# The opening of a transformer layer on TensorE: matmuls in the order the program is written, against an order chosen by a scheduler

## The chip, the cores and the metric

The kernel runs on one core of a Trainium2 chip. The core has a matrix engine (TensorE, PE in the profile), a vector engine (DVE), a scalar engine (ACT), GpSimd (POOL) and SyncE (SP), which here only issues DMA transfers. Each engine works off its own list of instructions in order and waits on semaphores for the others. The metric is the device time of one execution in microseconds. Three runs of the kernel before took 2039.68, 2039.70 and 2042.13 us, median 2039.7 us.

## The reference

One layer of a hybrid model over 256 latent tokens `x` and 256 context tokens `ctx`, model width 2048, everything in fp32. Cut to what bears on this case:

```
mod_x = split(silu(c)     @ w_mod + b_mod, 6)      # shift, scale, gate, ... for x
mod_c = split(silu(c_ctx) @ w_mod + b_mod, 6)      # the same for ctx
modulate(x, g, shift, scale) = rms_norm(x, g) * (1 + scale) + shift
h   = modulate(x,   g_mix, mod_x[0], mod_x[1])
hc  = modulate(ctx, g_mix, mod_c[0], mod_c[1])
qa, ka, va, qb, kb, vb, rb, lrf, lrb, gate_a, gate_b = split(h  @ w_in, ...)
...                                             split(hc @ w_in, ...)
o_attn = windowed attention(qa, ka, va, context keys and values)
o_gla  = chunked bidirectional gated linear attention(qb, kb, vb, gates; starts from context end states)
x = x + mod_x[2] * (sigmoid(gate_a) * (o_attn @ w_attn_o) + sigmoid(gate_b) * (o_gla' @ w_gla_o)) @ w_out
x = x + mod_x[5] * conv_ffn(modulate(x, g_ffn, mod_x[3], mod_x[4]))
```

The modulation of each token by shift and scale needs the matrix product `silu(c) @ w_mod` first, and it needs the whole row of a token for the rms. So the first projection of `h` waits for both.

## The kernel before

**Numbers.** An fp32 operand is split into a high part and the rest (`hi` by ACT, `lo` by DVE), and each product is three matmuls: hi by hi, lo by hi, hi by lo. A weight tile of two k-tiles (256 rows by 512 columns, 512 KB) comes by a load into a `raw` buffer; `wsplit` (L156) makes `whi` (ACT) and `wlo` (DVE, 128x1024) from it.

**The opening**, about 213 us, runs from the start to the first gated-linear-attention (GLA) work. First `c` and `c_ctx` (`crow`) go through SiLU and a transpose (`pc`, L97). `load_tokens` (L356) loads the two 128-token tiles of a stream, sums squares (ACT L368 for the first tile, DVE L366 for the second, both into `junk`) and transposes them on TensorE (`ptx`, L373) into `xr`; the copies out of PSUM alternate between ACT (L378) and DVE (L376). `rms_scale` and `token_rows` turn the sums into a factor per token (DVE L330 to L344 with `dg` last, TensorE `pr` L345, ACT `rrow` L347). `mod_both` (L229) makes shift and scale for some k-tiles of both streams: 1 MB tiles of `w_mod` (`mraw`), matmuls `pm` (L245), a DVE transpose `mtr` (L248), a small matmul `pcol` (L250), four copies (L253), the bias (L256). `affine_group` (L398) makes `h` for some k-tiles: scale (L400), then for each k-tile DVE `xr` (L394), ACT hi (L395), DVE lo (L396). In names such as `h10lo` the first digit is the stream (0 is x, 1 is ctx).

The projections are made in groups of k-tiles, (first k-tile, count): (0,2), (2,2), (4,4), (8,4), (12,4). In each group the program writes: affine of x; the GLA queries of x in two blocks of 512 columns (QB, by `proj_T` L186); affine of ctx; the GLA keys of both streams (KB, `proj_T`); the values of both (VB, `proj_nat` L163). The partial sums of the groups are added up in `qb0`, `kb0` and `vb0` by `add_to` (L406): an ACT copy in the first group (L410), a DVE addition (L412) in the later ones. The modulation of the next group is cut into steps, and `tick()` (L133) takes one now and then at the rate `bg_rate`.

**What sets the order.** Loads on SP are chained in the order they are written (L66). On the compute engines a scheduler of the framework orders the instructions by a priority that follows the order of writing, and by what it expects to be ready; the weight splits have a high priority (L158). So the order in which the code is written is not the order on an engine.

**After the opening** come the columns of the convolution weights (L449 to L452), the low-rank gate projection (`plr`), the last block of GLA keys beside the first GLA head, then the heads, attention, the merge and the ConvFFN.

Of the kernel before, what the change touches and what calls it, by code (L numbers as in the profile page):

```python
# [30 lines left out]
def layer_kernel(ctx, tc, A, out):  # L31
# [44 lines left out]


    x00 = M("x00", [P, D])
    nc.sync.dma_start(x00, A["x"][0][0:P, :])
# [22 lines left out]
    def columns(name, parts, eng=G):  # L102
        rows = sm.tile([P, P], F32, name="rows", tag="t128", bufs=2)
        n = 0
        for ap in parts:
            k = ap.shape[0] // P
            eng.dma_start(rows[n:n + k, :], ap.rearrange("(k p) -> k p", p=P))
            n += k
        pt = bank("pt_" + name, (P, P))
        PE.transpose(pt[:, :n], rows[:n, :], ident[:n, :n])  # L110
        t = cst.tile([P, n], F32, name=name)
        V.tensor_copy(t, pt[:, :n])
        return t

    c1 = columns("c1", [A["b_mod"][0], A["g_mix"][0], A["g_ffn"][0]], nc.scalar)
    bmod, gmix, gffn = c1[:, 0:96], c1[:, 96:112], c1[:, 112:128]


    bg_steps = []
# [13 lines left out]
    def tick():  # L133
# [3 lines left out]
        while later and later[0][0] < 0:  # L137
            later.pop(0)[1]()
# [16 lines left out]

    def wsplit(src):  # L156
        raw = wload(src)
# [7 lines left out]
    def proj_nat(w, r0, c0, kts, lhs, evac):  # L165

        banks = [acc.tile([P, 512], F32, name="acc", tag="acc") for _ in lhs]
        for k0 in kts[::2]:
            tick()
            nk = min(2, kts[-1] + 1 - k0)  # L170
            hi, lo = wsplit(w[r0 + k0 * P:r0 + (k0 + nk) * P, c0:c0 + 512])
            for i, l in enumerate(lhs):
                for k in range(nk):
                    kt = k0 + k
                    ahi, alo = l(kt)
                    PE.matmul(banks[i], ahi, hi[:, k, :], start=(kt == kts[0]), stop=False)  # L176
                    PE.matmul(banks[i], alo, hi[:, k, :], start=False, stop=False)  # L177
            for i, l in enumerate(lhs):
                for k in range(nk):
                    kt = k0 + k  # L180
                    PE.matmul(banks[i], l(kt)[0], lo[:, k, :], start=False, stop=(kt == kts[-1]))  # L181
# [3 lines left out]
    def proj_T(w, c0, kts, rhs, evac):  # L185
# [4 lines left out]
        for k0 in kts[::2]:  # L190
            tick()
            nk = min(2, kts[-1] + 1 - k0)
            hi, lo = wsplit(w[k0 * P:(k0 + nk) * P, c0:c0 + 512])
            for part in range(2):
                for f in range(4):
                    for k in range(nk):
                        kt = k0 + k
                        w_ = (lo if part else hi)[:, k, f * P:(f + 1) * P]
                        for i, r in enumerate(rhs):
# [3 lines left out]
                            PE.matmul(o, w_, ahi, start=(kt == kts[0] and b == 0 and part == 0),  # L203
                                      stop=(kt == kts[-1] and part == 1), skip_group_check=True)
                            if part == 0:
                                PE.matmul(o, w_, alo, start=False, stop=False, skip_group_check=True)  # L206
        for i in range(len(banks)):
            evac(i, banks[i])
# [22 lines left out]
    def mod_both(part, t0, n, dst):  # L231
# [5 lines left out]
        def step(k0):  # L237
# [8 lines left out]
            if k0 == KT - nk:  # L246
                tr = W2("fb", "mtr", [P, n, 4, 32])
                V.transpose(tr.rearrange("p a b c -> p (a b c)"), a[0])  # L248
                pc = bank(f"pcol{part}_{t0}", (32, n * 4, 2))
                PE.matmul(pc, sel[:, 0:32], tr.rearrange("p a b c -> p (a b) c")[:, :, 0:2], start=True, stop=True)  # L250
                pv = pc.rearrange("p (a b) c -> p b c a", b=4)
                for b4 in range(4):
                    V.tensor_copy(dst[32 * b4:32 * b4 + 32, :, t0:t0 + n], pv[:, b4, :, :])  # L253
                b0 = part * 16 + t0
                d = dst[:, :, t0:t0 + n]
                V.tensor_tensor(d, d, bmod[:, b0:b0 + n].unsqueeze(1).to_broadcast([P, 2, n]), op=ALU.add)  # L256

        return [lambda k0=k0: step(k0) for k0 in range(0, KT, nk)]
# [92 lines left out]
    groups = [(0, 2), (2, 2), (4, 4), (8, 4), (12, 4)]  # L351
    mods = [mod_both(0, t0, n, shift1) + mod_both(1, t0, n, scale1) for t0, n in groups]
# [4 lines left out]

    def load_tokens(s):
        ss = sm.tile([P, 2], F32, name="ss0", tag="ss0", bufs=2)
        for t in range(2):  # L360
            x_ = x00
            if s or t:
                x_ = M(f"x{s}{t}", [P, D])
                load(x_, A["ctx" if s else "x"][0][t * P:(t + 1) * P, :])
            if t:
                V.scalar_tensor_tensor(junk, x_, 1.0, x_, op0=ALU.mult, op1=ALU.mult, accum_out=ss[:, t:t + 1])  # L366
            else:
                S.activation(junk, x_, AF.Square, accum_out=ss[:, t:t + 1])  # L368
            for g in range(4):
                pt = bank("ptx", (P, 4, P), side=True)  # L370
                for k in range(4):
                    kt = g * 4 + k
                    PE.transpose(pt[:, k, :], x_[:, kt * P:(kt + 1) * P], ident)  # L373
                dst = xr[2 * s + g // 2][:, (g % 2) * 4:(g % 2) * 4 + 4, t * P:(t + 1) * P]
                if g % 2:
                    V.tensor_copy(dst, pt)  # L376
                else:
                    S.activation(dst, pt, AF.Copy)  # L378
        rrow1.append(token_rows("fa", f"rrow{s}", rms_scale(ss, D, [P, 2])))
# [35 lines left out]
    hh, hl = [], []  # L415
    for gi, (t0, n) in enumerate(groups):
        kts = ALL[t0:t0 + n]
        if gi == 0:
            load_tokens(0)
            for f in mods[0]:  # L420
                f()
        while bg_steps:
            bg_steps.pop(0)()
        if gi + 1 < len(groups):
            bg_steps.extend(mods[gi + 1])
# [613 lines left out]
```

## Time and profile before

| | |
|---|---|
| median of three runs | 2039.7 us |
| the profiled execution's own time | 2039.47 us |
| its span in the trace | 2037.7 us |
| TensorE busy | 1979.4 us (97%) |
| DVE busy | 1430.0 us (70%) |
| ACT busy | 960.7 us (47%) |
| granted TensorE clock, mean | 0.991 |
| end of group (0,2) and of the opening in the trace | 62.98 us and 213.08 us |

The profile is of one execution. Times in the trace count from the start of the span, which is 1.8 us shorter than the execution's own time. Matmuls are pipelined, so the durations of single matmuls overlap, and the distance between two starts is what one costs. A granted clock of 1.00 is 2.4 GHz and 0.50 is 1.2 GHz. Where a row says `[3.23 <-DVE dg L344]`, the engine was idle for 3.23 us before it, and that instruction ended the wait.

### The profile page before, as it was taken

How to read it: one execution, taken by the hardware profiler on the slowest of the kernel's cores; microseconds unless marked ns; L12 is line 12 of the kernel's file. 1: busy time of each engine (PE TensorE's matmuls, PEld its weight loads, DVE VectorE, ACT ScalarE, POOL GpSimd, SP SyncE). 2: the span in 40 equal slices, each digit the busy share in tenths (PEclk: the TensorE clock that was granted, in tenths of full speed). 3: DMA queues.
4: the chain of work that ended last, by engine and by line, in shares of the span. 5: the costliest groups of instructions: out<-in, count | busy, mean ns of one | idle time of the engine just before them, and what ended most of it. 6: DMA issues, size and time to landing. Idle time of an engine off the chain costs nothing.

```text
span 2037.7 us, 27395 instructions
## 1 busy us (share of the span) xinstructions
PE 1979.4 (97%) x10384; PEld 1647.3 (81%) x10384; DVE 1430.0 (70%) x2237; ACT 960.7 (47%) x1394; POOL 38.9 (2%) x62
## 2 busy tenths in 40 slices
PE   6999999999999999999999999899999999999998
PEld 4778888888787777787778888788888888888887
DVE  4657577887758888877775455788887555667754
ACT  4323464553345656444334444565555434556532
POOL 0001000001000000000000000000000000000000
PEclk8999999999999999999999999899999999999999
DMA  9977223345544456788886665577776656555563
GB/s 350 364 259 224 91 77 93 93 135 192 172 146 129 124 184 206 263 271 272 273 269 220 237 207 187 193 248 251 261 245 207 212 193 193 188 187 187 193 211 111
DMA packets 214340, 413.54 MB, mean 203 GB/s; under 512 B 12548, under 2 KB 21092, under 8 KB 213184
## 3 DMA queue, kind: packets, MB, share of 16 engines
q1 hardware_dynamic: 212320, 406.89, 60.5%
q0 software_dynamic: 1360, 4.74, 0.8%
q8 instruction: 81, 1.33, 0.3%
q14 instruction: 51, 0.42, 0.1%
q10 hardware_dynamic: 528, 0.17, 0.0%
HBM read 409.63 MB, written 2.11 MB: 202 GB/s over the span
## 4 chain that ended last, share of the span: by engine, by line
PE 78%; DVE 10%; DMA 8%; ACT 2%; issue 2%; DVEq 0%; POOL 0%; ACTq 0%; SPq 0%
PE acc L176 13%; PE acc L177 13%; PE acc L181 13%; PE acc L219 8%; PE accs L219 8%; DMA raw<-in_w_mod 8%; PE acc L223 4%; PE accs L223 4%; PE acc L203 3%; DVE wlo L62 3%; DVE macc L284 3%; PE acc L206 2%; PE pm L245 1%; PE pa L552 1%; ACT whi L61 1%
## 5 line engine op out<-in xcount | busy, mean ns | idle before, releaser
L61 ACT ACTIVATE whi<-raw 128x1024 fp32r<-128x1024 f32 x568 | 600.9, 1059 | 784.7 <-PE acc L177 500.7
L62 DVE TENSOR_TENSOR wlo<-raw,whi 128x1024 fp32r<-128x1024 f32 x568 | 694.1, 1226 | 335.4 <-ACT whi L61 302.6
L284 DVE SCALAR_TENSOR_TENSOR macc<-raw,ccol,macc 128x512 f32<-128x512 f32 x240 | 180.3, 751 | 110.5 <-DMA raw<-in_w_mod 107.0
L219 PE MATMUL acc<-h,whi 128*128 128x512 f32 x704 | 178.6, 396 | 2.2 <-DVE h L396 2.2
L219 PE MATMUL accs<-h,whi 128*128 128x512 f32 x704 | 176.3, 392 | 0.0
L219 PEld LDWEIGHTS acc<-h,whi 128*128 128x128 f32 x704 | 127.8, 191 | 25.6 <-DVE h L396 2.5
L219 PEld LDWEIGHTS accs<-h,whi 128*128 128x128 f32 x704 | 126.6, 189 | 22.6
L176 PE MATMUL acc<-whi,h00hi 128*128 128x512 f32 x352 | 141.2, 401 | 1.5 <-DVE kb L412 0.6
L176 PE MATMUL acc<-whi,h01hi 128*128 128x512 f32 x352 | 139.8, 397 | 0.0
L177 PE MATMUL acc<-whi,h00lo 128*128 128x512 f32 x352 | 139.8, 397 | 0.0
L177 PE MATMUL acc<-whi,h01lo 128*128 128x512 f32 x352 | 137.7, 391 | 0.0
L177 PE MATMUL acc<-whi,al 128*128 128x512 f32 x352 | 137.1, 389 | 0.0
L176 PE MATMUL acc<-whi,ah 128*128 128x512 f32 x352 | 137.0, 389 | 0.0
L223 PEld LDWEIGHTS acc<-h,wlo 128*128 128x128 f32 x704 | 97.0, 192 | 7.1
L223 PEld LDWEIGHTS accs<-h,wlo 128*128 128x128 f32 x704 | 96.0, 190 | 6.9
L223 PE MATMUL acc<-h,wlo 128*128 128x256 f32 x704 | 99.1, 284 | 0.0
L181 PE MATMUL acc<-wlo,h00hi 128*128 128x512 f32 x352 | 98.0, 394 | 0.2 <-DVE wlo L62 0.2
L223 PE MATMUL accs<-h,wlo 128*128 128x256 f32 x704 | 98.2, 282 | 0.0
L181 PE MATMUL acc<-wlo,h01hi 128*128 128x512 f32 x352 | 97.0, 393 | 0.0
L181 PE MATMUL acc<-wlo,ah 128*128 128x512 f32 x352 | 94.4, 389 | 0.0
L176 PEld LDWEIGHTS acc<-whi,h00hi 128*128 128x128 f32 x352 | 66.9, 190 | 15.6 <-ACT kb L410 0.7
L181 PEld LDWEIGHTS acc<-wlo,h00hi 128*128 128x128 f32 x352 | 65.8, 189 | 14.4 <-DVE wlo L62 1.0
(375 smaller groups left out, 3461.5 us busy)
## 6 DMA issues: line engine op xcount, KB each, us to landing
raw<-in_w_in SPq DMA_DIRECT2D x208, 512.0 KB, 4.1
raw<-in_w_up SPq DMA_DIRECT2D x176, 512.0 KB, 3.6
raw<-in_w_mod SPq DMA_DIRECT2D x128, 512.0 KB, 4.0
raw<-in_w_down SPq DMA_DIRECT2D x88, 512.0 KB, 3.7
mraw<-in_w_mod SPq DMA_DIRECT2D x32, 1024.0 KB, 11.9
raw<-in_w_attn_o SPq DMA_DIRECT2D x32, 512.0 KB, 4.5
raw<-in_w_gla_o SPq DMA_DIRECT2D x32, 512.0 KB, 4.7
raw<-in_w_out SPq DMA_DIRECT2D x32, 512.0 KB, 3.6
```

Of the source, the lines that this page charges most:

```text
L61: S.activation(hi, src, AF.Copy)
L62: V.tensor_tensor(lo, src, hi.bitcast(F32), op=ALU.subtract)
L176: PE.matmul(banks[i], ahi, hi[:, k, :], start=(kt == kts[0]), stop=False)
L177: PE.matmul(banks[i], alo, hi[:, k, :], start=False, stop=False)
L181: PE.matmul(banks[i], l(kt)[0], lo[:, k, :], start=False, stop=(kt == kts[-1]))
L203: PE.matmul(o, w_, ahi, start=(kt == kts[0] and b == 0 and part == 0), stop=(kt == kts[-1] and part == 1), skip_group_check=True)
L206: PE.matmul(o, w_, alo, start=False, stop=False, skip_group_check=True)
L219: PE.matmul(banks[f], hi[:, k, f * P:(f + 1) * P], pair(k0 + k), start=(k0 + k == kts[0]), stop=False, skip_group_check=True)
L223: PE.matmul(banks[f][:, 0:T], lo[:, k, f * P:(f + 1) * P], pair(k0 + k)[:, 0, :], start=False, stop=(k0 + k == kts[-1]), skip_group_check= ...
L245: PE.matmul(a[0][q:q + 32, :], cS[:, kt, :], raw[:, k, :], start=(kt < 4), stop=(kt >= 12))
L284: V.scalar_tensor_tensor(a[0], raw[:, k, :], ccol[:, kt:kt + 1], a[0], op0=ALU.mult, op1=ALU.add)
L552: PE.matmul(pa[:, t, :], k2[:, dt, t * P:(t + 1) * P], q2[:, dt, tq * P:(tq + 1) * P], start=(dt == 0), stop=(dt == 1))
```

## The change

The opening's matmuls are put on TensorE in the order in which the code is written (`tc.manual_schedule` for PE alone, closed behind the last group); the other engines are still ordered by the scheduler. The written order is new too:

- the two tiles of x are loaded first and in one chain, and both are transposed before the modulation;
- the end of a modulation (`pcol`, copies, bias) is a step of its own, and 34 transposes of the identity into an otherwise unused PSUM bank (`warm`, `keep_busy`) are written between the steps of the first modulation;
- the weight tiles of the first QB blocks, and of the first VB and KB, are loaded ahead (`early`);
- the context is loaded before the first QB, and transposed behind it;
- VB stands before KB, and KB is last in every group;
- the groups are (0,2), (2,2), (4,2), (6,2), (8,4), (12,4): one more than before;
- `tick()` is called after every 6 or 12 matmuls instead of every weight tile, and `proj_nat` takes the four token tiles in two pairs;
- the first of the four convolution columns (`cw0`) moves ahead of the last group.

```diff
+    order = ExitStack()
+    order.enter_context(tc.manual_schedule(engines={mybir.EngineType.PE}))
...
-        while later and later[0][0] < 0:
-            later.pop(0)[1]()
+        due = [e for e in later if e[0] < 0]
+        later[:] = [e for e in later if e[0] >= 0]
+        for e in due:
+            e[1]()
...
     def wsplit(src):
-        raw = wload(src)
+        raw = early.pop(0) if early else wload(src)
...
+            step = 2 if fine[0] else len(lhs)
+            for i2 in range(0, len(lhs), step):
+                for part in range(2):
+                    for i in range(i2, min(i2 + step, len(lhs))):
...
+                            if fine[0] and mms % 6 == 0 and mms < len(lhs) * nk * 3:
+                                tick()
...
-    groups = [(0, 2), (2, 2), (4, 4), (8, 4), (12, 4)]
-    mods = [mod_both(0, t0, n, shift1) + mod_both(1, t0, n, scale1) for t0, n in groups]
+    groups = [(0, 2), (2, 2), (4, 2), (6, 2), (8, 4), (12, 4)]
+    def both_parts(t0, n):
+        (s0, e0), (s1, e1) = (mod_both(part, t0, n, dst) for part, dst in ((0, shift1), (1, scale1)))
+        if n == 4:
+            s0, s1 = ([lambda f=s[i], g=s[i + 1]: (f(), g()) for i in (0, 2)] for s in (s0, s1))
+        return s0 + s1[:1] + [e0] + s1[1:] + [e1]
...
+    warm = acc.tile([P, 512], F32, name="warm", tag="acc")
+    def keep_busy(n):
+        for _ in range(n):
+            PE.transpose(warm[:, 0:P], ident, ident)
+    first = both_parts(*groups[0])
+    x_t = load_tokens(0)
+    turn_tokens(0, 0, x_t[0])
+    turn_tokens(0, 1, x_t[1])
+    turn_c1()
+    first[0]()
+    first[1]()
+    token_factor(0)
+    keep_busy(8)
+    first[2]()
+    keep_busy(8)
+    first[3]()
+    first[4]()
+    keep_busy(8)
+    first[5]()
+    keep_busy(10)
+    for j in range(2):
+        early.append(wload(w_in[0:256, QB + j * 512:QB + j * 512 + 512]))
...
         if gi + 1 < len(groups):
-            bg_steps.extend(mods[gi + 1])
-            ticks = 4 * ((n + 1) // 2)
-            bg_rate[:] = [1.4 * len(bg_steps) / ticks + 0.01, 0.0]
...
+            more = both_parts(*groups[gi + 1])
+            bg_rate[:] = [(2.0 if gi == 0 else 1.4) * len(more) / (6 * n), 0.0]
+            if gi:
+                bg_steps.extend(more)
+        affine_group(0, t0, n)
+        if gi == 0:
+            x_t = load_tokens(1)
+        for j in range(2):
+            proj_T(w_in, QB + j * 512, kts, [h_all(0)], add_to(lambda i, j=j: qb0[2 * j + i], gi == 0))
         if gi == 0:
+            for c in (VB, KB):
+                early.append(wload(w_in[0:256, c:c + 512]))
+            turn_tokens(1, 0, x_t[0])
+            turn_tokens(1, 1, x_t[1])
+            more[0]()
+            token_factor(1)
+            new_h(1)
+            bg_steps.extend(more[1:])
             kbt = M("kb0", [P, 4, 512])
             vb0 = M("vb0", [P, 4, 512])
+        affine_group(1, t0, n)
+        proj_nat(w_in, 0, VB, kts, h_xc, add_to(lambda i: vb0[:, i, :], gi == 0))
         proj_T(w_in, KB, kts, [h_all(0), h_all(1)], add_to(lambda i: kbt[:, i, :], gi == 0))
-        proj_nat(w_in, 0, VB, kts, h_xc, add_to(lambda i: vb0[:, i, :], gi == 0))
+        if gi == len(groups) - 2:
+            chain.clear()
+            cw0, turn_cw0 = columns("cw0", [A["conv_w"][0, 0], A["b_gate_f"][0], A["b_gate_b"][0]])
...
+            defer(8, gate_bias)
+    flush()
+    fine[0] = False
+    order.close()
```

On TensorE, from the first transposes to the first query matmul, the list before reads (`x16` is sixteen of a kind; the numbers in names count tiles):

```order
L373 MATMUL ptx<-ident,x_147 128x128 x16
L345 MATMUL pr<-dg,ones 128x128 x2
L245 MATMUL pm_0_193<-mraw,cS 32x256 x16
L250 MATMUL pcol_0_216<-mtr,sel 32x16
L245 MATMUL pm_0_223<-mraw,cS 32x256 x16
L250 MATMUL pcol_0_246<-mtr,sel 32x16
L245 MATMUL pm_2_270<-mraw,cS 32x256 x8
L203 MATMUL acc<-h00hi,whi 128x256
```

The same stretch of the changed kernel:

```order
L412 MATMUL ptx<-ident,x_121 128x128 x16
L115 MATMUL pt_c_174<-ident,rows 128x128
L272 MATMUL pm_0_177<-mraw,cS 32x256 x16
L375 MATMUL pr<-dg,ones 128x128 x2
L467 MATMUL warm<-ident 128x128 x8
L272 MATMUL pm_0_227<-mraw,cS 32x256 x8
L467 MATMUL warm<-ident 128x128 x8
L280 MATMUL pcol_0_246<-mtr,sel 32x16
L272 MATMUL pm_0_227<-mraw,cS 32x256 x8
L467 MATMUL warm<-ident 128x128 x8
L280 MATMUL pcol_0_273<-mtr,sel 32x16
L467 MATMUL warm<-ident 128x128 x10
```

The first modulation's sixteen matmuls now stand ahead of `pr`, the half of the next modulation (`pm_2_270`) no longer stands ahead of the queries, and the filling transposes are in between.

On DVE, from the copies of the first scale to the first `h00lo` and the context's copies, before:

```order
L253 COPY scale_111<-pcol_0_246 32x2x2 x4
L256 TENSOR_TENSOR scale_111<-scale_111,c_108 128x2x2
L400 SCALAR_TENSOR_TENSOR scale_111<-scale_111,c_108 128x2 x2
L394 SCALAR_TENSOR_TENSOR xr_116<-xr_116,scale_111,rrow_191 128x256 x2
L396 SCALAR_TENSOR_TENSOR h00lo<-xr_116,shift_110,h00hi 128x256 x2
L62 TENSOR_TENSOR wlo<-raw,whi 128x1024
L248 STREAM_TRANSPOSE mtr<-pm_2_270 128x256
L62 TENSOR_TENSOR wlo<-raw,whi 128x1024
```

and in the changed kernel:

```order
L283 COPY scale_108<-pcol_0_273 32x2x2 x4
L62 TENSOR_TENSOR wlo<-raw,whi 128x1024
L286 TENSOR_TENSOR scale_108<-scale_108,c_106 128x2x2
L441 SCALAR_TENSOR_TENSOR scale_108<-scale_108,c_106 128x2 x2
L435 SCALAR_TENSOR_TENSOR xr_113<-xr_113,scale_108,rrow_217 128x256
L62 TENSOR_TENSOR wlo<-raw,whi 128x1024
L437 SCALAR_TENSOR_TENSOR h00lo<-xr_113,shift_107,h00hi 128x256
L435 SCALAR_TENSOR_TENSOR xr_113<-xr_113,scale_108,rrow_217 128x256
L437 SCALAR_TENSOR_TENSOR h00lo<-xr_113,shift_107,h00hi 128x256
L405 SCALAR_TENSOR_TENSOR junk,ss_309<-x_311 128x2048
L415 COPY xr_115<-ptx 128x4x128
L62 TENSOR_TENSOR wlo<-raw,whi 128x1024
```

Two weight splits (`wlo`) have moved from behind `h00lo` to ahead of it, and the context's sum of squares (`junk`) stands before the first of its copies.

On DVE at the seam between the groups (6,2) and (8,4) of the changed kernel, with the additions of the keys (`kb_466`) and the `h01` of the next group:

```order
L286 TENSOR_TENSOR scale_108<-scale_108,c_106 128x2x4
L441 SCALAR_TENSOR_TENSOR scale_108<-scale_108,c_106 128x4 x2
L435 SCALAR_TENSOR_TENSOR xr_114<-xr_114,scale_108,rrow_217 128x256 x2
L453 TENSOR_TENSOR kb_466<-kb_466,acc 128x512 x4
L437 SCALAR_TENSOR_TENSOR h01lo<-xr_114,shift_107,h01hi 128x256 x2
L435 SCALAR_TENSOR_TENSOR xr_114<-xr_114,scale_108,rrow_217 128x256 x2
```

The first `h01lo`, which the queries of group (8,4) read, stands behind the four additions of the group before.

## Rows read from the trace of the kernel before

**Rows 1.** The page: busy time of each engine, and TensorE's clock in 40 slices.

```profile
PE 1979.4 (97%) x10384; PEld 1647.3 (81%) x10384; DVE 1430.0 (70%) x2237; ACT 960.7 (47%) x1394; POOL 38.9 (2%) x62
...
PEclk8999999999999999999999999899999999999999
```

**Rows 2.** Stretches of the opening: length, busy of each engine, clock, DMA, GB/s.

```profile
0.00:8.22 8.22, 0.00 (x0) 0.00 (x0) 0.65 (x2) 1.62 (x3) 0.88 (x5) 1.00 0.77 257
8.22:28.67 20.45, 13.18 (x122) 8.86 (x123) 10.90 (x36) 8.07 (x13) 0.00 (x0) 0.92 1.08 353
28.67:62.98 34.31, 28.88 (x209) 23.81 (x209) 18.32 (x43) 15.90 (x29) 2.09 (x4) 0.90 1.04 378
62.98:90.78 27.80, 25.57 (x189) 17.95 (x188) 19.16 (x40) 9.22 (x14) 0.00 (x0) 1.00 0.97 352
90.78:134.26 43.48, 43.48 (x310) 34.07 (x309) 27.06 (x54) 13.64 (x20) 0.00 (x0) 1.00 0.84 309
134.26:178.56 44.30, 43.44 (x310) 33.96 (x309) 30.34 (x58) 12.62 (x17) 6.89 (x11) 1.00 0.81 254
178.56:213.08 34.52, 34.24 (x242) 32.12 (x242) 21.39 (x27) 10.87 (x12) 0.00 (x0) 1.00 0.54 168
```

**Rows 3.** TensorE's timeline from 12 to 64 us: start, duration, instructions, idle before.

```profile
12.98 1.53 PE L373 MATMUL ptx<-ident,x 128*128 128x128 f32 x12 [0.24 <-DVE xr L376]
17.74 0.68 PE L345 MATMUL pr<-dg,ones 128*128 128x128 f32 x4 [3.23 <-DVE dg L344]
...
24.81 0.23 PE L250 MATMUL pcol<-mtr,sel 128*32 128x16 f32 x2 [0.56 <-DVE mtr L248]
24.91 1.07 PE L245 MATMUL pm<-mraw,cS 128*32 128x256 f32 x16
28.67 0.38 PE L203 MATMUL acc<-h00hi,whi 128*128 128x256 f32 x1 [2.69 <-ACT whi L61]
...
38.01 1.47 PE L373 MATMUL ptx<-ident,x 128*128 128x128 f32 x12
45.83 0.98 PE L345 MATMUL pr<-dg,ones 128*128 128x128 f32 x4 [3.03 <-DVE dg L344]
...
57.31 0.50 PE L176 MATMUL acc<-whi,h00hi 128*128 128x512 f32 x1 [0.54 <-ACT kb L410]
```

**Rows 4.** The three stretches of the opening at half clock, columns as in rows 2.

```profile
18.80:22.10 3.30, 2.85 (x28) 1.09 (x20) 0.40 (x1) 0.05 (x1) 0.00 (x0) 0.50 1.09 348
...
29.10:32.40 3.30, 3.30 (x17) 3.30 (x17) 0.78 (x1) 0.00 (x0) 0.00 (x0) 0.50 1.04 421
...
46.10:49.40 3.30, 3.30 (x32) 1.70 (x35) 1.76 (x4) 1.99 (x4) 2.09 (x4) 0.50 1.04 385
```

**Rows 5.** DVE's timeline, 25 to 46 us.

```profile
25.08 0.65 DVE L253 COPY scale<-pcol 32x4 f32<-32x4 f32 x4 [0.33 <-PE pcol L250]
...
27.30 0.88 DVE L396 SCALAR_TENSOR_TENSOR h00lo<-xr,shift,h00hi 128x256 fp32r<-128x256 f32 x2 [0.18 <-ACT h00hi L395]
28.65 1.23 DVE L62 TENSOR_TENSOR wlo<-raw,whi 128x1024 fp32r<-128x1024 f32 x1 [0.46 <-ACT whi L61]
...
41.13 2.28 DVE L366 SCALAR_TENSOR_TENSOR junk<-x 128x2048 f32<-128x2048 f32 x1
...
45.40 0.48 DVE L344 TENSOR_SCALAR dg<-ident,rstd 128x128 f32<-128x128 f32 x2
```

**Rows 6.** ACT's timeline, 32 to 37 us.

```profile
32.86 1.08 ACT L410 ACTIVATE qb<-acc 128x512 f32<-128x512 f32 x2 [4.24 <-PE acc L203]
...
34.77 1.92 ACT L368 ACTIVATE junk<-x 128x2048 f32<-128x2048 f32 x1
```

**Rows 7.** What TensorE waited for behind the opening, 213 to 300 us.

```profile
PE pa L552 <- DVE q L572: 1.5, 1, 1.5
PE pa L617 <- DVE kf L610: 1.0, 1, 1.0
```

**Rows 8.** DVE to 213 us by form: busy, mean ns, idle before.

```profile
L412 DVE TENSOR_TENSOR kb<-kb,acc 128x512 f32<-128x512 f32 x16 | 10.2, 683 | 4.0 <-PE acc L203 4.0
```

More of the change, by code (lines that the diff above doesn't have):

```diff
@@ L171, in proj_nat @@
             hi, lo = wsplit(w[r0 + k0 * P:r0 + (k0 + nk) * P, c0:c0 + 512])
[L172 to L181, printed above, removed]
+            mms = 0
+            step = 2 if fine[0] else len(lhs)
+            for i2 in range(0, len(lhs), step):
+                for part in range(2):
+                    for i in range(i2, min(i2 + step, len(lhs))):
+                        for k in range(nk):
+                            kt = k0 + k
+                            ahi, alo = lhs[i](kt)
+                            first, last = kt == kts[0], kt == kts[-1]
+                            if part == 0:
+                                PE.matmul(banks[i], ahi, hi[:, k, :], start=first, stop=False)
+                                PE.matmul(banks[i], alo, hi[:, k, :], start=False, stop=False)
+                                mms += 2
+                            else:
+                                PE.matmul(banks[i], ahi, lo[:, k, :], start=False, stop=last)
+                                mms += 1
+                            if fine[0] and mms % 6 == 0 and mms < len(lhs) * nk * 3:
+                                tick()
         for i in range(len(lhs)):
@@ L193, in proj_T @@
             hi, lo = wsplit(w[k0 * P:(k0 + nk) * P, c0:c0 + 512])
+            mms = 0
             for part in range(2):
@@ L248, in step, with end @@
                 V.transpose(tr.rearrange("p a b c -> p (a b c)"), a[0])
[L249 to L258, printed above, removed]
+                a.append(tr)
+        def end():
+            pc = bank(f"pcol{part}_{t0}", (32, n * 4, 2))
+            PE.matmul(pc, sel[:, 0:32], a[1].rearrange("p a b c -> p (a b) c")[:, :, 0:2], start=True, stop=True)
+            pv = pc.rearrange("p (a b) c -> p b c a", b=4)
+            for b4 in range(4):
+                V.tensor_copy(dst[32 * b4:32 * b4 + 32, :, t0:t0 + n], pv[:, b4, :, :])
+            b0 = part * 16 + t0
+            d = dst[:, :, t0:t0 + n]
+            V.tensor_tensor(d, d, bmod[:, b0:b0 + n].unsqueeze(1).to_broadcast([P, 2, n]), op=ALU.add)
+        return [lambda k0=k0: step(k0) for k0 in range(0, KT, nk)], end
     def mod_latent(parts, put=lambda fn: defer(3, fn)):
@@ L356, in layer_kernel, with turn_tokens, token_factor @@
     junk = M("junk", [P, D])
+    sums = {}
     def load_tokens(s):
-        ss = sm.tile([P, 2], F32, name="ss0", tag="ss0", bufs=2)
+        sums[s] = sm.tile([P, 2], F32, name="ss0", tag="ss0", bufs=2)
+        tiles = [M(f"x{s}{t}", [P, D]) for t in range(2)]
         for t in range(2):
[L361 to L366, printed above, removed]
-            else:
[L368 to L379, printed above, removed]
+            load(tiles[t], A["ctx" if s else "x"][0][t * P:(t + 1) * P, :])
+        return tiles
+    def turn_tokens(s, t, x_):
+        ss = sums[s]
+        if t:
+            V.scalar_tensor_tensor(junk, x_, 1.0, x_, op0=ALU.mult, op1=ALU.mult, accum_out=ss[:, t:t + 1])
+        else:
+            S.activation(junk, x_, AF.Square, accum_out=ss[:, t:t + 1])
+        for g in range(4):
+            pt = bank("ptx", (P, 4, P), side=True)
+            for k in range(4):
+                kt = g * 4 + k
+                PE.transpose(pt[:, k, :], x_[:, kt * P:(kt + 1) * P], ident)
+            dst = xr[2 * s + g // 2][:, (g % 2) * 4:(g % 2) * 4 + 4, t * P:(t + 1) * P]
+            if g % 2:
+                V.tensor_copy(dst, pt)
+            else:
+                S.activation(dst, pt, AF.Copy)
+    def token_factor(s):
+        rrow1.append(token_rows("fa", f"rrow{s}", rms_scale(sums[s], D, [P, 2])))
     def h_tok(s, t):
```

62 lines of the change are left out of this document (31 added, 31 removed).

## The prediction

> **What bounds the kernel now.** I read the page first: TensorE is busy for 97% of the span and its clock is full almost everywhere [rows 1], so what can be gained are the places where it idles or runs at half clock. Next, the stretches of the opening, which the change rewrites. The reader is to see there how much each lacks of a full TensorE: 20.45 - 13.18 = 7.3 us from 8.22 to the first query matmul, 34.31 - 28.88 = 5.4 us in group (0,2), and 2.2, 0, 0.9 and 0.3 us in the four groups behind it, 3.4 us in all [rows 2]. So the gain to be had lies in the first 63 us. TensorE's timeline says what it waits for there: 3.23 us for the `dg` of x, 2.69 us for the first weight split, 3.03 us for the `dg` of the context, some half microseconds at each `pcol` [rows 3]. Last, the clock: three stretches of 3.3 us stand at 0.50, that is 1.2 GHz, each of them behind one of the holes, all other stretches of the opening at 2.4 GHz [rows 4]. A stretch of 3.3 us at half clock does 1.65 us of work and so costs 1.65 us where TensorE is busy; the first was busy for 2.85 and cost 1.4. Together 4.7 us.
>
> DMA runs at 353 to 378 GB/s there [rows 2], but it is not the limit of the new opening: 2.1 MB are in by 8.22 (257 GB/s), and the first modulation needs x, four 1 MB tiles and some constants, about 6.5 MB. The remaining 4.4 MB take 12.5 us at 353 GB/s: the last tile is there by 20.7 us, earlier than the matmuls below want it.
>
> **Part one: from the start to the first queries.** Removed from the path are the two pieces of the next modulation that stood before and between the query blocks, 1.07 us each [rows 3]; they come later and count there. The first sixteen `pm` go into the hole before `pr`. `pr` itself comes at about 18.6 instead of 17.74, since DVE now has two PSUM copies of the opening (about 0.9 us with their waits) ahead of the rms. Behind `pr` (0.5) follow in fixed order 8 fillers, 8 `pm`, 8 fillers, `pcol`, 8 `pm`, 8 fillers, `pcol`. A filler is a 128x128 transpose like those of x, 12 records in 1.53 us, 0.12 each [rows 3], so 0.95 a pack; a piece of `pm` is 1.0. That makes 18.6 + 0.5 + 0.95 + 1.0 + 0.95 + 0.1 + 1.0 + 0.95 = 24.0 for the second `pcol`. Without the last pack it would wait for its `mtr` until 23.65, so the fillers cost 0.35; the rest of them lies in waits. Before, this `pcol` stood at 24.81: 0.8 gained.
>
> But the gain is lost on DVE, which works in the order shown. Copies end at 24.95; then comes the `wlo` (1.23 [rows 5]) that stood behind `h00lo` before, then bias and scale until 26.6, `xr` 27.0, the second `wlo` until 28.2, the first `h00lo` 28.65, and the second pair until 29.6. Before, from the copies' start to the end of both `h00lo` it was 28.18 - 25.08 = 3.1 us [rows 5]; now it is 29.6 - 24.3 = 5.3, the two splits being 2.3 of that. The queries run freely from about 30.1, against 28.67. In exchange both splits are done, so nothing waits inside the blocks: 48 matmuls at 0.12, 5.9 us. TensorE idles from 25.2 to about 28.7, so I put half clock behind it as before, of which about 1.0 us costs. The end is at 37.0, against 38.01 with 2.1 us of `pm` in it: 1.1 us lost in work. Bounds: 27.4 (24.3 + 3.1) for the queries if the splits hide, 31 if a split also waits for its high part.
>
> **Part two: the context, to the end of group (0,2).** The square of the first context tile stands on ACT behind the copies of the first query block (34.0 + 1.1), as before [rows 6], and ends at 37.0. DVE's `junk` writes the same buffer, waits for it, and takes 2.28 [rows 5], to 39.3. Only then come the four copies (0.65 each) with two `wlo` (1.2 each) in between, and some waits for the high parts: 44.8. From the last copy to `pr` it is 1.1 us before, plus what is queued; I take `pr` at 46.6, against 45.83. TensorE, which has one piece of `pm` for this hole, idles for some 5 us and goes on at half clock. Behind `pr` (0.5): three pieces of `pm` (3.0), the half-clock loss (1.65), `pcol` (0.3): VB starts at 52.0. VB is 5.5 us (57.31 to 62.98 before [rows 3], less its slow start) and KB, 48 matmuls like those of the queries, 5.9, with 0.5 for the first waits in them: 63.9 to 64.2, against 62.98 for the same work. **+1.2 us.** Bounds: 62.0, with no half clock and no wait in VB and KB, and 66.6, where each `wlo` between the copies waits for one more ACT instruction (2.1) and the seam for 0.3.
>
> **Part three: the five groups behind it.** The matmuls are the same in number. One more group adds 12 additions on DVE, at 683 ns [rows 8] 8.2 us, and two ends of modulation; in a group of two k-tiles DVE has then some 19.6 us of work beside 21 us of matmuls, so these hide, and would cost up to 8.2 us without that cover (second rival). New is the wait at a seam. KB is last, its four additions can begin when its first bank is done, 1.4 us before the block ends (12 matmuls of 0.12), and take 4 x 0.62 = 2.5 (683 ns each [rows 8], less what two in a row overlap): they end 1.1 us behind the last key matmul. Where `h..lo` of the next queries stands behind them, TensorE waits 1.1 us and the `lo` (0.4 each). By DVE's order this is one `lo` at the start of (4,2), 1.1 us; none at (6,2), 0.2; both at (8,4), 2.0; a split at (12,4), 0.4. Together 3.7, against the 3.4 us of idle time that stand there now and whose waits (values behind the keys) go with the new order: **+0.3 us**. Bounds: -3.4, if all idle time goes, and +4.0, if each seam takes 1.85.
>
> **Part four: behind the opening.** The rest of the program keeps its order. Only `plr`, 16 matmuls (1.9 us), stands earlier against the keys beside the first GLA head, which leaves as much more work to cover the two waits there, 1.5 and 1.0 us [rows 7]. I take **-1.6 us**, between 0 (they wait for DVE, which is no earlier) and -2.5.
>
> **Sum.** 1.2 + 0.3 - 1.6 = -0.1 us: 2039.4 us against the profiled execution's own 2039.47, 0.2 below the median of the runs. I say 2039 us. All lower ends together give 2032.6, all upper ones 2047; as they are independent, the forecast's own range is 2035 to 2043.5. A measurement of this kernel tells about 0.2%, 4.1 us, from no change.
>
> **Rivals.** First, the written order closes the holes: DVE and ACT keep pace, queries begin at 27.4, and the context is transposed at TensorE's pace. Then from the queries' start to the end of group (0,2) only the work is left: 5.9 + 3.5 (`ptx`) + 0.6 + 3.9 (`pm`) + 5.5 + 5.9 = 25.3, with 1.65 of half clock an end at 54.3, 8.6 us earlier: 2039.5 - 8.6 + 0.3 - 1.6 = 2029.5. For it: half of DVE and ACT time up to 63 us is free [rows 2]. Against it: they work in order, and what is late stands ahead of what is wanted. Half of it would give 2035. Chance 0.21.
>
> Second, slower: at the four seams the additions do not overlap with the last keys, because DVE comes late to them with 93% load. Each seam then costs 2.5 + 0.4 = 2.9 us, 11.6 - 3.4 = 8.2: 2039.5 + 1.2 + 8.2 - 1.6 = 2047.3. It decides (over +4.1) from 2.0 us a seam on. For it: in before the `kb` additions make DVE wait for TensorE by only 4.0 us in 16 [rows 8], so they are close to back to back; against it: the modulations are ready long before. Chance 0.16.
>
> Third, the fillers hold the clock. The three slow stretches each followed a hole of some 3 us [rows 4, 3]; if TensorE's fillers count as work and the holes get short, the 1.0 and 1.65 us in parts one and two go: 2036.7. Chance 0.12. The Trainium skill, "TensorE: Matmul & The Clock Gate", section "What's actually happening", says that the slow state is the default and that activity releases it, which speaks for this rival; the rows agree as far as the slow stretches stand behind idle time, and whether transposes of the identity are activity in this sense no row of before shows.
>
> Fourth, the order is kept but the context's chain falls to its upper bound, with half clock behind it: 66.6, 2042. Chance 0.05.
>
> **Chances.** My forecast 0.46. Faster by over 0.2%: the first rival nearly whole (0.19), a part of the third (0.04) and of the forecast's lower tail (0.08): 0.31. Slower: the second (0.14), 0.02 of the fourth, and the forecast's upper tail (0.06): 0.22. Same: 0.47. The range that holds the time 8 times in 10 reaches to the first rival's half and a little over, and to the second's beginning: 2031 to 2045.
>
> **What would show it.** Right: the first query matmul free from 30 us, waits on `h00lo` before it; `pr` of the context at 46 to 47 behind `dg`; group (0,2) ending near 64; waits for `h..lo` at (4,2) and (8,4); less than 1 us left at `pa` in the first head. Wrong: queries before 28.5, a context `pr` before 43, no half clock at all, or seams of over 2 us each. A group (0,2) that ends before 59 would make the forecast wrong by more than its own range.

## The result, and the profile after

The changed kernel took 2048.4 us (median of 11 runs, 2041.71 to 2052.75), the kernel before 2039.68 us (11 runs, 2035.85 to 2043.03). The ratio is 1.0036 with a 95% interval of 1.0025 to 1.0047: 7.3 us slower, 5.1 to 9.6. The prediction was 2039 us, with 2031 to 2045 as its range. It was wrong.

The profiled execution of the changed kernel is the shortest of its 11 runs: 2041.71 us (span 2039.9, mean clock 0.993; the runs at 0.990 took 2048.4 to 2052.75). So its trace can't be compared by its end. I compare at one point of the work instead: the first output matmul of the first GLA head (`po`), at 284.06 us before and at 288.38 after. A second profile of the same kernel (the first experiment) has it at 289.94, so two traces of one kernel can lie 1.6 us apart there.

The stretches after, with the columns of [rows 2] (length; busy us and number of instructions of TensorE, its weight loads, DVE, ACT and GpSimd; granted clock; DMA share; GB/s), cut at the first matmul, the first query, the end of group (0,2), the end of the opening, and `po`:

```profile
0.00:10.79 10.79, 0.00 (x0) 0.03 (x1) 0.65 (x2) 2.92 (x4) 0.88 (x5) 1.00 0.85 250
10.79:30.08 19.29, 15.96 (x141) 12.13 (x141) 11.29 (x34) 7.64 (x12) 0.00 (x0) 1.00 1.06 372
30.08:65.81 35.73, 29.95 (x226) 24.59 (x226) 18.82 (x46) 16.29 (x30) 2.09 (x4) 0.90 1.08 356
65.81:217.76 151.95, 149.07 (x1115) 119.98 (x1113) 106.68 (x202) 45.09 (x61) 7.13 (x12) 1.00 0.80 263
217.76:288.38 70.62, 68.79 (x618) 62.99 (x617) 52.19 (x99) 36.02 (x71) 5.33 (x6) 1.00 0.29 84
```

The kernel before, cut at the end of its opening and at `po`:

```profile
0.00:213.08 213.08, 188.79 (x1375) 150.78 (x1376) 127.81 (x254) 71.94 (x105) 9.86 (x20) 0.98 0.85 294
213.08:284.06 70.98, 68.47 (x617) 62.98 (x616) 53.25 (x101) 36.72 (x72) 5.42 (x7) 1.00 0.27 84
```

The reader should add up TensorE's busy time, the first figure behind the length. Before it is 257.3 of 284.1 us, so 26.8 us idle; after it is 263.8 of 288.4, 24.6 us idle. **TensorE waits 2.2 us less than before, and is busy 6.5 us longer.** In the second profile it waits 26.6 us, hardly less than before, and is busy 6.0 us longer. The kernel got slower with no more waiting than before; most of the added busy time is the filling transposes (the run without them, below).

Where it starts, and what it waits for in the first 55 us (TensorE's timeline after; start, duration, instructions, idle before):

```profile
10.79 0.28 PE L98 MATMUL pc<-ident,crow 32*128 32x32 f32 x1 [10.79 <-DMA ident<-in_k_ident]
...
20.91 0.71 PE L375 MATMUL pr<-dg,ones 128*128 128x128 f32 x4 [1.10 <-DVE dg L374]
...
26.51 0.24 PE L280 MATMUL pcol<-mtr,sel 128*32 128x16 f32 x2
26.68 1.31 PE L467 MATMUL warm<-ident 128*128 128x128 f32 x10
30.08 0.45 PE L226 MATMUL acc<-h00hi,whi 128*128 128x256 f32 x1 [2.09 <-ACT h00hi L436]
31.07 0.58 PE L227 MATMUL acc<-h00lo,whi 128*128 128x256 f32 x1 [0.54 <-DVE h00lo L437]
...
48.97 0.71 PE L375 MATMUL pr<-dg,ones 128*128 128x128 f32 x4 [2.27 <-DVE dg L374]
...
54.36 0.50 PE L194 MATMUL acc<-whi,h00hi 128*128 128x512 f32 x1
```

The first row is new. Before, the first matmul waited for ACT until 8.22; now it waits for the identity matrix until 10.79. From the issue of that 64 KB load (`ident`) to its landing it is 9.0 us (the profile's list of DMA issues, 0 to 16 us, us in the last column):

```profile
ident<-in_k_ident ACTq DMA_DIRECT2D x1, 64.0 KB, 9.0
```

and in the kernel before 5.3 us:

```profile
ident<-in_k_ident ACTq DMA_DIRECT2D x1, 64.0 KB, 5.3
```

While it was on its way the DMA rate fell: from 5.5 to 7.0 us (columns as above), first in the changed kernel, then in the kernel before.

```profile
5.50:7.00 1.50, 0.00 (x0) 0.00 (x0) 0.00 (x0) 0.00 (x0) 0.00 (x0) 1.00 1.10 89
5.50:7.00 1.50, 0.00 (x0) 0.00 (x0) 0.00 (x0) 0.43 (x1) 0.00 (x0) 1.00 1.10 365
```

DVE after, 27 to 49 us, answers to [rows 5]: both splits stand ahead of the last `h00lo`, and `junk` ahead of the context's copies.

```profile
27.47 1.23 DVE L62 TENSOR_TENSOR wlo<-raw,whi 128x1024 fp32r<-128x1024 f32 x1
...
29.40 1.22 DVE L62 TENSOR_TENSOR wlo<-raw,whi 128x1024 fp32r<-128x1024 f32 x1
...
31.99 0.48 DVE L437 SCALAR_TENSOR_TENSOR h00lo<-xr,shift,h00hi 128x256 fp32r<-128x256 f32 x1 [0.58 <-ACT h00hi L436]
39.86 2.29 DVE L405 SCALAR_TENSOR_TENSOR junk<-x 128x2048 f32<-128x2048 f32 x1 [7.39 <-ACT junk L407]
...
48.62 0.48 DVE L374 TENSOR_SCALAR dg<-ident,rstd 128x128 f32<-128x128 f32 x2
```

TensorE's waits from the end of group (0,2) to the end of the opening: two, 2.8 us, at the seams.

```profile
PE acc L227 <- DVE h01lo L437: 1.6, 1, 1.6
PE acc L227 <- DVE h00lo L437: 1.2, 1, 1.2
```

And a cut in the values (group (2,2), TensorE). Read the distances between starts: in the row of matmuls 0.23 us, at 76.17 0.32 to the `pcol` put in between, 0.16 for that, and 0.34 from the first matmul behind it to the second. The cut itself costs 0.09 + 0.11 = 0.2 us beside the work that it lets in, and no idle time is shown for it.

```profile
75.94 0.39 PE L194 MATMUL acc<-whi,h00hi 128*128 128x512 f32 x1
76.17 0.39 PE L195 MATMUL acc<-whi,h00lo 128*128 128x512 f32 x1
76.49 0.23 PE L280 MATMUL pcol<-mtr,sel 128*32 128x16 f32 x2
76.65 0.50 PE L194 MATMUL acc<-whi,h00hi 128*128 128x512 f32 x1
76.99 0.39 PE L195 MATMUL acc<-whi,h00lo 128*128 128x512 f32 x1
77.22 1.09 PE L198 MATMUL acc<-wlo,h00hi 128*128 128x512 f32 x4
```

Half clock stood from 30.0 to 36.8 behind the queries' waits (the two stretches below, columns as in [rows 4]), and nowhere else in the opening: 6.8 us against 9.9 before.

```profile
30.00:33.40 3.40, 2.42 (x7) 1.64 (x8) 1.90 (x4) 0.53 (x2) 0.00 (x0) 0.54 1.05 374
33.40:36.80 3.40, 3.40 (x18) 3.40 (x18) 0.00 (x0) 0.24 (x1) 0.00 (x0) 0.50 1.09 348
```

### The profile page after: what moved, and what is told of

It reads as the page before. It is cut to its first block, busy times and chain, and to the rows that moved or that the text cites. A ratio compares the mean times of both kernels' runs of the same rounds, so it can differ in the third digit from the quotient of the medians.

```text
span 2039.9 us, 27622 instructions
## 1 busy us (share of the span) xinstructions
PE 1982.6 (97%) x10486; PEld 1652.6 (81%) x10486; DVE 1437.2 (70%) x2263; ACT 959.5 (47%) x1394; POOL 38.3 (2%) x62
## 4 chain that ended last, share of the span: by engine, by line
PE 78%; DVE 9%; DMA 8%; ACT 2%; issue 2%; DVEq 0%; ACTq 0%; POOL 0%; SPq 0%
PE acc L194 13%; PE acc L195 13%; PE acc L198 13%; PE acc L246 8%; PE accs L246 8%; DMA raw<-in_w_mod 7%; PE acc L250 4%; PE accs L250 4%; DVE wlo L62 3%; DVE macc L314 2%; PE acc L226 2%; PE acc L227 2%; PE acc L230 2%; PE pm L272 1%; PE pa L635 1%
## 5 line engine op out<-in xcount | busy, mean ns | idle before, releaser
L246 PEld LDWEIGHTS acc<-h,whi 128*128 128x128 f32 x704 | 127.6, 190 | 25.5 <-DVE h L437 2.5
L194 PEld LDWEIGHTS acc<-whi,h01hi 128*128 128x128 f32 x352 | 66.4, 189 | 13.9 <-issue 0.8
```

The costliest lines, as they stand in the source:

```text
L194: PE.matmul(banks[i], ahi, hi[:, k, :], start=first, stop=False)
L246: PE.matmul(banks[f], hi[:, k, f * P:(f + 1) * P], pair(k0 + k), start=(k0 + k == kts[0]), stop=False, skip_group_check=True)
```

## Experiments

Ratios are to the kernel before, run on the same chip, with 95% intervals; 0.0005 is 1 us. A difference between two runs' ratios carries the intervals of both, about 0.0016 or 3 us together. So what a single part gave by its ratio, 2 to 3 us below, is not clear of noise by the time alone; it needs the trace beside it, and there the two profiles of the unchanged kernel lie 1.6 us apart at `po`. Theory A of the expectations says that fixed waits of the opening cost, theory B that only the clock differs.

**The change again, unchanged.**

> The changed kernel once more, unchanged, for a second profile. Theory A (fixed waits of the opening cost 4 to 5 us, and the first profile, with 29 us at half clock against 35 before, hid part of it): the opening again ends about 2.4 us later at the low-rank gate matmuls (221.9 against 219.6), or more where the clock falls more often, and runs with the same mean clock as before are 5 to 7 us slower than before. Theory B (only the clock differs): the new profile has more half-clock stretches than the first, and its time follows their number alone; with as many as before it would take 2040 us.

Median 2047.6 us, ratio 1.0041 (1.0026 to 1.0055). Mean clocks of its runs were 0.990 to 0.993, those of the kernel before beside it 0.988 to 0.992; at one clock, 0.991, it took 2047.6 us (one execution) and the kernel before 2037.7 to 2043.5. The profiled execution, at 0.992, had the higher mean clock than the profile before (0.991) and took 7.1 us longer. Theory B falls. `po` came at 289.94, 5.9 us later than before, with TensorE busy 263.3 us and idle 26.6.

```profile
0.00:289.94 289.94, 263.29 (x2093) 219.47 (x2094) 189.56 (x380) 108.19 (x176) 15.36 (x27) 0.99 0.71 236
```

**The second tile of x later.**

```diff
+            if s == 0 and t == 1:      # the load of x01 waits for the first DMA of c
+                tc.add_manual_dep(chain[-1], crow_in.ins.name, ... Sync ...)
```

> The changed kernel with one wait added: the load of the second tile of x waits for the first DMA of c, as it happened to in the kernel before; all orders stay. Theory A: the identity matrix lands 3 to 4 us earlier, the first transpose starts at about 8.2 instead of 10.8 us, and 2 to 2.6 us of it reach the end: ratio 0.9988 to the changed kernel, about 2046 us. Theory B: no change of the median within 1 us.

Median 2045.86, ratio 1.0027 (1.0015 to 1.0039): 2.5 us below the change by the medians, 1.8 by the ratios, with overlapping intervals. The trace shows the start directly; `ident` landed after 5.3 us:

```profile
8.28 0.31 PE L98 MATMUL pc<-ident,crow 32*128 32x32 f32 x1 [8.28 <-ACT crow L91]
...
18.43 0.71 PE L375 MATMUL pr<-dg,ones 128*128 128x128 f32 x4 [1.40 <-DVE dg L374]
...
45.99 0.71 PE L375 MATMUL pr<-dg,ones 128*128 128x128 f32 x4 [2.27 <-DVE dg L374]
```

Each of these rows stands 2.5 to 3.0 us earlier than in the change, and `po`, at 286.07, 2.3 us earlier than in its first profile.

**The kernel before with that load alone.** Both tiles of x are issued at the start.

```diff
     nc.sync.dma_start(x00, A["x"][0][0:P, :])
+    x01 = M("x01", [P, D])
+    nc.sync.dma_start(x01, A["x"][0][P:2 * P, :])
```

> The kernel before with one part of the change alone: the second tile of x is loaded at once. If that load pushes the identity matrix back: first transpose at 10.8 instead of 8.2 us and 2 to 2.6 us slower, 2042 us. If the late identity has to do with the change's other loads: the same as before.

Median 2043.3 us, ratio 1.0015 (1.0007 to 1.0024): 3 us slower than before, with nothing else of the change. The first matmul, and the stretch to `po` (at 287.38, 3.3 us later than before):

```profile
11.07 0.28 PE L99 MATMUL pc<-ident,crow 32*128 32x32 f32 x1 [11.07 <-DMA ident<-in_k_ident]
0.00:287.40 287.40, 257.24 (x1991) 213.81 (x1992) 181.30 (x354) 108.90 (x177) 15.31 (x27) 0.98 0.70 238
```

TensorE is busy 257.2 us, as before; the 3.3 us are waiting. The load issued early costs this, in both kernels. All 18 traces agree on the landing of `ident`: 8.9 to 9.6 us from its issue in the ten that issue both tiles of x at once, 4.9 to 5.4 us in the eight that don't.

**No fillers.**

```diff
-        for _ in range(n):
+        for _ in range(n * 0):
             PE.transpose(warm[:, 0:P], ident, ident)
```

> The changed kernel without the 34 filling transposes. If they hold the clock: half clock appears between 20 and 30 us and the first queries, and the time grows by 1.5 to 3.5 us. If they only lie in waits and delay the second modulation by one pack: 0.3 to 1 us faster in the opening, same time.

Median 2047.72, ratio 1.0038 (1.0025 to 1.0050): the same time. To `po`, here at 289.0, TensorE was busy 258.7 us instead of 263.8 and idle 30.3 instead of 24.6. The fillers turned waiting into busy time. They didn't hold the clock either in this pair of traces: without them it is full from 18 to 29 us, and half for about as long behind the queries' wait.

```profile
0.00:289.00 289.00, 258.72 (x2058) 216.16 (x2059) 189.33 (x380) 108.06 (x176) 15.58 (x27) 0.99 0.71 237
18.00:29.00 11.00, 5.37 (x73) 2.84 (x73) 8.14 (x30) 3.81 (x7) 0.00 (x0) 1.00 1.05 388
29.80:36.40 6.60, 6.45 (x31) 6.45 (x32) 0.49 (x2) 1.74 (x3) 0.00 (x0) 0.52 1.07 361
```

**TensorE ordered by the scheduler.** First with the fillers, then without.

```diff
-    order.enter_context(tc.manual_schedule(engines={mybir.EngineType.PE}))
```

> The changed kernel with TensorE's opening ordered by the scheduler again; what is written stays. If the fixed order of TensorE is what costs (theory C): 4 to 7 us faster, near 2041 us. If the written order on the other engines and the loads cost (theory A): still 2045 us or more.

> The changed kernel without fillers and with TensorE's opening ordered by the scheduler: the run with the scheduler had the fillers ahead of the first transpose, which this one can't have. If the fixed order of TensorE costs by itself: 2044 us or less, against 2047.7 without fillers in fixed order. If it gains: 2050 us or more. If neither: 2047 to 2049.

With the fillers 2051.02 us, 1.0054 (1.0037 to 1.0071): the scheduler put them ahead of the first transpose, at 11.22 us, and that came at 14.19; so this run says nothing on the order. Without them 2048.86, 1.0045 (1.0030 to 1.0060), against 1.0038 in fixed order: neither gains.

**Cuts at whole weight tiles only.**

```diff
-            bg_rate[:] = [(2.0 if gi == 0 else 1.4) * len(more) / (6 * n), 0.0]
+            bg_rate[:] = [(2.0 if gi == 0 else 1.4) * len(more) / (2 * n) + 0.01, 0.0]
...
-                            if fine[0] and mms % 6 == 0 and mms < len(lhs) * nk * 3:
+                            if cut[0] and mms % 6 == 0 and mms < len(lhs) * nk * 3:      # cut = [False]
```

> The changed kernel with the modulation's pieces between the projection blocks only at whole weight tiles, as before the change, instead of after every 6 or 12 matmuls. If the cuts cost (each leaves 0.2 us more between matmuls; the values take 46.5 instead of 44.3 us of TensorE): 1.5 to 2.5 us faster, about 2046 us, values back to 44.5. If the cuts are free, or the waits for the DVE transposes come back (4.8 us before): 2048 us or up to 2051.

Median 2044.42, ratio 1.0026 (1.0013 to 1.0038). The projections were cut 15 times instead of 24 (19 in the kernel before). To `po` TensorE was busy 262.3 us; the matmuls of the values took 45.0 us from start to start, 46.5 in the change and 44.3 in the kernel before. The waits for `mtr` rose from 1.5 to 3.4 us and those for `h00lo` and `h01lo` fell from 3.3 to 0.4; `po` at 287.28, 1.1 and 2.7 us earlier than in the two profiles of the change.

**Keys before values.**

```diff
-        proj_nat(w_in, 0, VB, kts, h_xc, ...)
         proj_T(w_in, KB, kts, [h_all(0), h_all(1)], ...)
+        proj_nat(w_in, 0, VB, kts, h_xc, ...)
```

> The changed kernel with keys before values in every group, as before the change. If the seams behind the keys cost what the trace shows (1.2 us at group (4,2), 1.6 at (8,4)): these waits go and the time falls by 2 to 3 us, to about 2045.5. If another wait takes their place (values behind keys: 1.1 us in the kernel before): within 1 us of 2048.

Median 2045.97, ratio 1.0029 (1.0017 to 1.0041). The seam waits did not go, they moved: `h00lo` 3.9 us in four places and `h01lo` 1.2, against 1.7 in two places and 1.6 in the change. `po` at 288.58, between the two profiles of the change. Whether the median's 2.4 us are real this run doesn't say.

**Five groups.**

```diff
-    groups = [(0, 2), (2, 2), (4, 2), (6, 2), (8, 4), (12, 4)]
+    groups = [(0, 2), (2, 2), (4, 4), (8, 4), (12, 4)]
```

> The changed kernel with the five groups of before. If DVE's 12 additional sums and the additional modulation hide behind TensorE: the same within 1 us. If they don't: 2 to 4 us faster, about 2045.

Median 2044.16, ratio 1.0023 (1.0011 to 1.0036): the second expectation. In the trace it is 18 cuts instead of 24 and 0.9 us less at `pcol`; `po` at 287.66. So if the sixth group costs something, part of it is its cuts, the same as in the run on cuts.

**Splits behind.** Order on DVE alone, no new wait.

```diff
+        if behind[0] is not None:      # last h00lo for the queries' splits, the context's dg for the next two
+            tc.add_manual_dep(d.ins, behind[0].name, ... NoSync ...)
```

> The changed kernel with the weight splits on DVE in the first group moved: the two of the queries behind the first h00lo, the two of the next blocks behind the context's dg. By the sum of the prediction (2.3 us in front of the queries, 2.4 us between the context's copies): the first query starts at about 28.5 instead of 30.1 and both its parts are there, the context's pr at about 45 instead of 49, and the time falls by 3 to 4 us, to about 2044.5. If the waits only change place (the queries then wait for wlo, the values for theirs): 0 to 1.5 us.

Median 2044.25, ratio 1.0022 (1.0010 to 1.0034). The queries begin at 29.12, with 1.04 us of idle time before them instead of 2.09, and run on; the context's `pr` stands 6 us earlier than in the change, but the wait for `mtr` behind it, which stands behind the splits now, grew from 0.95 to 2.1, and `po`, at 286.81, is 1.6 and 3.1 us earlier than in the two profiles of the change:

```profile
29.12 0.38 PE L231 MATMUL acc<-h00hi,whi 128*128 128x256 f32 x1 [1.04 <-ACT h00hi L441]
...
42.95 0.71 PE L380 MATMUL pr<-dg,ones 128*128 128x128 f32 x4 [1.13 <-DVE dg L379]
...
47.64 0.20 PE L285 MATMUL pcol<-mtr,sel 128*32 128x16 f32 x1 [2.11 <-DVE mtr L280]
```

**The parts together.** Four undone (second x, cuts, groups, splits); those without fillers; the four and keys first with fillers; all five without.

> The changed kernel with four of its parts undone together: the second tile of x waits for c, the modulation is cut in only at whole tiles, five groups, splits behind h and behind dg. If each costs what it costs alone (medians: 2.5, 4.0, 4.2 and 4.1 us against 2048.4, or 2.1, 2.6, 3.7 and 2.5 at one clock): 2034 to 2038 us, faster than the kernel before. If they share one wait: 2041 to 2044.

> The same without the 34 filling transposes. If they lie in waits: the same within 1 us as with them. If they hold the clock, now that the holes are short: half clock between 20 and 30 us and 1.5 to 3 us slower. If they delay: up to 1 us faster.

> The four, and keys before values in every group as well. By the run with that alone (2.4 us of the median, 1.1 at one clock): 1 to 2 us faster than the four; if the splits and the seams were the same wait: no change.

> The changed kernel with five parts undone (second tile of x waits, whole-tile cuts, five groups, splits behind, keys first) and without fillers; what stays of the change is TensorE's fixed order, the early weight tiles and the context behind the queries. If no fillers (3.2 us) and keys first (3.7 us, both against four undone) add up: 2035 us, faster than before by 4. If they took away the same wait: 2038 us.

Four undone: 2041.77, ratio 1.0010 (0.9999 to 1.0020). Alone, by their ratios, the four were worth 1.8 + 2.0 + 2.7 + 2.9 = 9.4 us, more than the 7.3 there are; together they gave 5.3. Cuts and groups are partly the same, and each term has its 3 us of noise. Without fillers: 2038.59, 0.9996 (0.9986 to 1.0007). With keys first and fillers: 2038.11, 0.9992 (0.9983 to 1.0001). Both: 2038.59, 0.9987 (0.9979 to 0.9996), faster than the kernel before by 2.7 us, and `po` at 281.21, 2.9 us earlier. On top of the four, taking out the fillers gave 2.9 us and keys first 3.7, both within noise of nothing, and they do not add up; the traces don't explain it. What is clear of noise is the whole: 1.0036 with all parts, 0.9987 with five undone and no fillers.

The clock tells more of the fillers here. With the four undone it is full with them until the queries are done, and half without them from before the queries on (first row with fillers, second without):

```profile
23.80:34.00 10.20, 8.70 (x70) 7.96 (x69) 5.25 (x14) 6.33 (x10) 0.00 (x0) 1.00 1.03 389
23.80:34.00 10.20, 7.13 (x34) 6.80 (x35) 5.04 (x13) 4.25 (x7) 0.00 (x0) 0.52 1.03 391
```

Yet `po` came at 282.51 with them and at 281.57 without. And with keys first too, half clock stands at the queries in both traces, with fillers from about 28 us and without from about 25.5. Each is one execution: whether fillers can hold the clock is open, and that they gain time no run shows. Without them TensorE also waits for tiles of `w_mod` in the four-undone trace, 0.82 and 1.83 us, a second place where it waits for DMA.

**Two last questions on that kernel.** A buffer of its own for the context's sum of squares, and the scheduler's order for TensorE.

```diff
-            V.scalar_tensor_tensor(junk, x_, 1.0, x_, ...)
+            V.scalar_tensor_tensor(M("junk2", [P, D]) if s else junk, x_, 1.0, x_, ...)
```

> The same, and the context's second sum of squares (DVE) writes a buffer of its own, so that it need not wait for ACT's. If that wait, as the prediction has it, holds up the context's chain: pr of the context 1 to 2 us earlier and 1 to 2 us less. If TensorE's transposes or DVE's place in the order hold it: no change.

> The same as the one with five parts undone and no fillers, but TensorE's opening ordered by the scheduler. If the fixed order gains by itself: slower than that one by 2 us or more. If it costs: faster by 2 or more. If neither: within 1.5 us.

Own buffer: 2037.71, 0.9986 (0.9977 to 0.9994); `junk` started at 36.35 instead of 36.85 and `pr` at 42.13 instead of 42.58: half a microsecond, no more. Scheduler: 2037.72, 0.9986 (0.9976 to 0.9997): in time the fixed order of TensorE is worth nothing by itself, though the mean clocks of these runs are mostly 0.992, and 0.990 in fixed order. This last trace is the only one with no half clock in the opening, which ends at 207.15:

```profile
0.00:207.15 207.15, 185.03 (x1374) 149.17 (x1375) 127.89 (x255) 72.20 (x105) 9.61 (x20) 1.00 0.87 302
```

## Why the prediction was wrong

**The step that failed** is in its first part: "DMA ... is not the limit of the new opening". It counted bytes and asked when the last weight tile lands. It did not ask what a small load waits behind when 2 MB of x are issued at once; the identity matrix, which every transpose needs, took 3.7 us longer to land, and the first matmul came 2.6 us later. Two runs show it, one by putting the wait back and one by taking it from the kernel before. The change named the place, since the load of x was one of the steps moved; the list of DMA issues was not among the rows that the prediction read.

**What was right**, taken from this start: the hand chain of parts one and two. `pr` of x was to be at 18.6, and stands at 18.43 with the wait back; the first queries waited for `h00lo` behind the two splits; the context's `pr` was to be at 46.6, and stands at 45.99 there; half clock came behind the queries' wait, though not behind the context's hole, where it was forecast too. The seams cost 2.8 us, two where they were named: (4,2) with 1.2 (forecast 1.1) and (8,4) with 1.6 (2.0).

**Part three** was mis-sized. From the end of group (0,2) to the end of the opening it was to be 0.3 us longer, and was 1.85 longer, while TensorE's idle time there fell from 3.4 to 2.9 us. The busy time grew by 2.3, of which 2.2 are the values' 46.5 us instead of 44.3: the sum took the matmuls as "the same in number" and priced none of the cuts between them. (They aren't the same in number, as 64 `pm` records of 128x512 became 128 of 128x256, but these cost the same: 8 of the one and 16 of the other take 1.00 us from start to start.) The trace of the kernel before has half of the cut's price: behind a piece of `pm` the second query matmul starts 0.22 us after the first, at 91.78 and 92.00, and the next ones 0.12. The sixth group's additions were costed at nothing, with 8.2 as the price without cover; removing the group gave 2.7 us by the ratio, within noise, and part of it in cuts. How much the additions themselves cost is not told apart.

**Part four** forecast -1.6 and the trace gives -0.4: the waits fell from 2.5 to 1.7 us [rows 7]. Both still end with DVE; why the 16 matmuls that moved ahead of them did not cover more, no run tells.

So at `po` the first profile is 4.3 us behind, where the sum had -0.1. The start was missing with 2.6, part three was 1.5 too low and part four 1.2, and parts one and two together, taken from the late start, were 0.9 too high.

In busy and idle time the 4.3 are 2.6 for the start and 6.5 of busy time, less 4.8 us of idle time behind the start. The fillers blur this: without them the idle time behind the start is 30.3 - 11.4 = 18.9 us, against 26.8 - 8.2 = 18.6 in the kernel before. So apart from laying fillers into the holes, the change took no waiting away.

In these traces nothing more is lost behind `po`. From there to the end of the span it is 1753.6 us before, and 1751.5 and 1754.8 in the two profiles of the change, with about 24, 22 and 26 us of half clock in these stretches; with half of that taken off (an estimate: a busy stretch at 0.50 does half of its work), the three agree within 1.2 us. In the opening the change had some 3 us less of half clock than the kernel before, worth some 1.5 us by the same estimate. At an equal clock `po` would thus be 6 and 7 us late in the two profiles, which is about the measured 7.3.

**Rivals.** The first wanted the queries at 27.4 and the end of group (0,2) at 54.3; they stand at 30.08 and 65.81, or 27.5 and 63.2 with the late start taken off, so the holes behind the queries' start did not close. The second, slower by seams, had the sign but not the mechanism: 2.8 us in all, where 2.0 a seam were wanted. The third falls for this change by the run without fillers, which has the same time and clock. The fourth had group (0,2) at its upper bound of 66.6; without the late start it is 63.2. The sentence of the Trainium skill that stands beside the third, that activity releases the slow clock ("TensorE: Matmul & The Clock Gate", "What's actually happening"), is neither borne out nor refuted by transposes of the identity here: in the change the clock is full with and without them and then half behind the same wait, and with four parts undone it is half without them only, which speaks for the sentence, in one pair of traces.

## What to carry to other kernels

When a load is issued earlier, list every small transfer that will share the DMA engines with it, above all constants that the first instruction needs; bytes per second don't show that. Price a reordering in busy time as well as in waits: each small piece put between two streams of matmuls cost 0.2 us here and shows as no wait, and the fillers raised the busy time by 5 us without a gain. On an engine that works in order, look at what the scheduler has placed ahead of the instruction that the critical engine waits for: moving four splits back brought the first queries 1 us and the context's `pr` 6 us earlier, though the time only by 3 us with as much noise.

## What was not expected of the hardware

A 64 KB load took 8.9 to 9.6 us instead of 4.9 to 5.4 when 2 MB were issued on another queue in the same microseconds. The mean rate was as high (250 GB/s to 10.79 us, against 257 to 8.22), but it fell to 89 GB/s from 5.5 to 7.0 us, while the small load was under way. And the time moves along with the mean clock by as much as this change: the one run of the changed kernel at 0.993 lies 7 to 11 us below the six at 0.990, and in the second batch the one at 0.993 lies 4 to 6 us below the two at 0.990. So a single profile can hide a result of 7 us.
